# Feed-forward down product: one sum over the inner dimension in eight PSUM banks, in place of Strassen groups

## The chip, the cores and the metric

The kernel runs on one core of a Trainium2 chip. The core has five engines that run beside one another: TensorE (PE) multiplies matrices, VectorE (DVE) and ScalarE (ACT) do elementwise work, GpSimd (POOL) does so too, and SyncE (SP) issues transfers. A matmul's result goes to PSUM, which has eight banks of 128 x 512 floats; everything else lies in SBUF, in tiles of 128 partitions. The metric is the device time of one execution in microseconds.

## The reference

Two layers, each a token mixer and a feed-forward block with a normalised residual after both. Only the feed-forward block is touched:

```python
def layer_norm(x, g, b, eps=LN_EPS):
    mu = x.mean(-1, keepdims=True)
    var = jnp.square(x - mu).mean(-1, keepdims=True)
    return (x - mu) * lax.rsqrt(var + eps) * g + b

def conv_ffn(x, w_up, conv_w, conv_b, w_down):
    S = x.shape[1]
    u = x @ w_up
    up = jnp.pad(u, ((0, 0), (CONV_W - 1, 0), (0, 0)))
    u = sum(up[:, j:j + S] * conv_w[j] for j in range(CONV_W)) + conv_b
    gate, val = jnp.split(u, 2, axis=-1)
    return (jax.nn.silu(gate) * val) @ w_down

for i in range(2):
    x = layer_norm(ALPHA * x + mixer[i](x), ...)          # RWKV, then sparse attention
    x = layer_norm(ALPHA * x + conv_ffn(x, ...), ...)
```

There are 1024 tokens, the model dimension is 1024 and the inner dimension of the feed-forward block 2816, which is 22 blocks of 128 or 11 pairs of blocks. All values are float32. The product at issue is the last one, silu(gate) * val (1024 x 2816) times w_down (2816 x 1024).

## The kernel before

The program has four phases, one after the other: RWKV mixer, feed-forward block of layer 0, sparse attention, feed-forward block of layer 1 (L1948 to L1953). Each is a generator, and `drive` (L1956) lets the next phase begin its first steps between the last steps of the one before. The order of the instructions on each engine and the places of the tiles are set by a scheduler from the order in which the code names them, from the pools' buffer counts and from estimates of its own.

A product in float32 precision is made of three matmuls (`mm3`, L63 to L67): each operand is split into a high part, which ScalarE casts (`split`, L54), and a low part, the rest, which VectorE or GpSimd subtracts (L60). L65 multiplies high by high, L66 and L67 high by low and low by high. A matmul has a 128 x 128 stationary operand and a 128 x 512 moving one.

In the feed-forward block the up product comes first (`up`, L1019, itself in Strassen form), then per block the convolution and the gate on ScalarE and VectorE (`conv` L1041, `gated` L1055). The gated values go to a scratch in DRAM, `hd`, one 512 KB block of 128 x 1024 for each inner block.

Then comes the down phase. Before, it takes the pairs in groups: three, three, two and two pairs in layer 0, and three times three in layer 1. Inside a pair the two blocks, the two halves of the tokens and the two halves of the columns form the 2 x 2 scheme of Strassen's product: seven products in place of eight. `d_load` brings a pair into a `raw` tile (L1146, L1147). `d_op` (L1152) makes the operands of one of the seven products with VectorE sums and differences (L1158, L919) and splits them into `dh` and `dl`. `down` makes the product for four token tiles and all pairs of the group in a bank, and `add_to` (L1177) adds the bank to `acc` in SBUF on VectorE. The inner blocks that no group holds, two in layer 0 and four in layer 1, are multiplied directly at the end (bank `dt`, tiles `to`), tile by tile, and each tile's last addition (L1271) is followed by its norm (`norm_store` L146, `layer_norm_rows` L80 to L111) and its store. The norm's reciprocal root (`lnrs`, L103) and its last products (L110, L111) are GpSimd's, L107 is ScalarE's, the rest VectorE's.

Buffers by tag: `big` has three places in pool P and four in L in layer 0, two and five in layer 1; `t` (`t4`) has twelve in P and six or seven in N; `bank` gives four PSUM banks from PX and four from PY.

Layer 0's block yields after its last group, and the attention phase's first work lies between the last tiles: it multiplies two weight matrices into `wqk` (loads `uk` L1330, evacuation L1341, split, stores L1345) and splits its projection's weight `win`. Its real start are the loads `xr` (L1321) of the rows that the feed-forward block has stored, their transposes (`pt`) and the first `win` matmul.

Of the kernel before, what the change touches and what calls it, by code (L numbers as in the profile page):

```python
# [7 lines left out]
F32 = mybir.dt.float32  # L8
# [6 lines left out]
D = 1024  # L15
# [879 lines left out]
def ffn(k, layer, src, dst):  # L895
# [236 lines left out]
            gated(f)  # L1132


    NPAIR = NF // 2
    cuts = [0, 3, 6, 8, 10] if layer == 0 else [0, 3, 6, 9]
    groups = [range(a, b) for a, b in zip(cuts, cuts[1:])]
    in_P = (0, 3, 4, 8, 9) if layer == 0 else (0, 3, 6, 8)
    tail = range(2 * cuts[-1], NF)
    acc = []  # L1140
    R = {}

    def d_load(p):
# [8 lines left out]
    def d_op(p, n, pool, lo_eng):  # L1152

        r = R[p]
        raw = r["raw"]
        if n == "S1":
            q = r["q"] = sm("q")
            nc.vector.tensor_tensor(q[:, 0], raw[:, 1], raw[:, 3], ALU.add)  # L1158
            sub(q[:, 1], raw[:, 5], raw[:, 4])
        elif n == "S2":  # L1160
            q = r["q"]
            sub(q[:, 0], q[:, 0], raw[:, 0])
            sub(q[:, 1], raw[:, 7], q[:, 1])
        elif n == "S3":
            sub(raw[:, 1:6:4], raw[:, 0:8:7], raw[:, 1:6:4])
        elif n == "S4":
            sub(raw[:, 2], raw[:, 2], r["q"][:, 0])
        elif n == "22":
            sub(raw[:, 6], raw[:, 6], r["q"][:, 1])
        hi, lo = t4("dh", F32R, pool, (128, 2, 512)), t4("dl", F32R, pool, (128, 2, 512))  # L1170
        r[n] = hi, lo
        at = {"11": slice(0, 5, 4), "12": slice(2, 7, 4), "S3": slice(1, 6, 4), "S4": slice(2, 8, 5), "22": slice(3, 7, 3)}
        split(k, raw[:, at[n]] if n in at else r["q"], hi, lo, "a", lo_eng)
# [5 lines left out]
    B_ = {}  # L1179

    def down(gi, n, tt):
        new = n in ("11", "12", "S1")
        x = n in ("11", "S2", "S3", "22")
        if new:
            B_[x, tt] = bank("dn", PX if x else PY)
        ps = B_[x, tt]
        tsl = slice(128 * tt, 128 * tt + 128)
        for j, p in enumerate(groups[gi]):
            hi, lo = R[p][n]
            mm3(  # L1190
                k, ps, (hi[:, 0, tsl], lo[:, 0, tsl]), (hi[:, 1], lo[:, 1]), new and j == 0,
                n in ("12", "S4", "22") and j == len(groups[gi]) - 1, skip_group_check=True,
            )
# [3 lines left out]
    for p in groups[0]:
        d_load(p)
    for hf in range(2):
        a = big("acc", L_, (128, 4, 1024), F32)  # L1200
        acc.append(a)
        for tt in range(4):
            nc.sync.dma_start(a[:, tt], src[(4 * hf + tt) * 128 : (4 * hf + tt + 1) * 128, :])
    ng = len(groups)
    dsteps = [(gi, n) for gi in range(ng) for n in ("11", "12", "S1", "S2", "S3", "S4", "22")]
    done = set()

    def d_ops(j):
        if j < len(dsteps) and j not in done:
            done.add(j)  # L1210
            gi, n = dsteps[j]
            for i, p in enumerate(groups[gi]):
                d_op(p, n, N_ if i == 2 else P_, CFG["dl0"][3 * j + i] if j < 3 else "v" if i == 2 and n in ("11", "12", "S4") else "p")

    hs = []

    def tail_op(f):

        if layer == 1 and f == NF - 1:
            room = [t4("to", F32R, N_) for _ in range(4)]  # L1220
        else:
            room = big("to", L_, (128, 4, 1024))
            room = [room[:, i] for i in range(4)]
        for i, ap in enumerate((hd[f // 2][f % 2], k.w_down[layer, f * 128 : (f + 1) * 128, :])):
            raw = t4("tr")
            nc.sync.dma_start(raw, ap)
            split(k, raw, room[2 * i], room[2 * i + 1], "a", "p")
        hs.append(room)

    late = [NF - CFG["gl"] + i for i in range(CFG["gl"])]  # L1230
    for j, (gi, n) in enumerate(dsteps):
        for x in CFG["ga"] if j == 0 else "":
            if x == "g":
                gated(late.pop(0))
            else:
                d_ops(int(x))
        d_ops(j)
        if n == "11" and gi + 1 < ng:
            for p in groups[gi + 1]:
                d_load(p)  # L1240
        d_ops(j + 1)
        if j == 0:
            while late:
                gated(late.pop(0))
        if gi == ng - 1 and n in ("S2", "S3", "S4") and (i := ("S2", "S3", "S4").index(n)) < len(tail):
            tail_op(tail[i])
        for tt in range(4):
            down(gi, n, tt)
    if len(tail) > 3:
        tail_op(tail[3])  # L1250
    lnw = []
    for z in range(2):
        if layer == 0:
            lnw.append(L_.tile([128, D], F32, name=f"lnw{z}"))
        else:
            lnw.append(sm("lnw").rearrange("p a b -> p (a b)"))
        i = B_LN + 4 * layer + 2 + z
        nc.sync.dma_start(lnw[z], k.bvec[i : i + 1, :].to_broadcast([128, D]))
# [3 lines left out]
    for tt in range(8):
        tsl = slice(128 * tt, 128 * tt + 128)
        r = [acc[tt // 4][:, tt % 4, 512 * ch : 512 * ch + 512] for ch in range(2)]
        sums = L_.tile([128, 2], F32, name="lns", tag="lns", bufs=2)
        for ch in range(2):
            cs = slice(512 * ch, 512 * ch + 512)
            ps = bank("dt")
            for i, (a, b, c, d) in enumerate(hs):
                mm3(k, ps, (a[:, tsl], b[:, tsl]), (c[:, cs], d[:, cs]), i == 0, i == len(hs) - 1)  # L1270
            nc.vector.scalar_tensor_tensor(  # L1271
                r[ch], r[ch], 1.0, ps, ALU.mult, ALU.add, accum_out=sums[:, ch : ch + 1]
            )
        kw = {} if layer else dict(sums=sums, junk=L_.tile([128, 512], BF16, name="lnj", tag="lnj", bufs=1))
        norm_store(k, L_, r, lnw, dst, 128 * tt, CFG["ln4"][layer] if tt < 7 else "pv", **kw)
# [711 lines left out]
```

## Time and profile before

| | us |
|---|---|
| median of 3 runs | 3228.42 (3226.88 to 3240.63) |
| the profiled execution | 3233.26 |
| its span on the core | 3231.4 |
| PE busy (15032 matmuls) | 2864.5, 89% |
| DVE busy | 2455.2, 76% |
| POOL busy | 1518.1, 47% |
| ACT busy | 1377.4, 43% |
| layer 0's down phase | about 1504 to 1805 |
| layer 1's down phase | about 2956 to 3231 |

The span is the time in which the core works; the rest of the execution's time lies around it. Times in the rows below count from the start of the span. A matmul's row says 0.39 us, since matmuls overlap in the array; the distance between starts is what one costs. "Idle before" in brackets is how long an engine waited ahead of an instruction and what released it. The granted clock is TensorE's as a share of its full 2.4 GHz.

### The profile page before, as it was taken

How to read it: one execution, taken by the hardware profiler on the slowest of the kernel's cores; microseconds unless marked ns; L12 is line 12 of the kernel's file. 1: busy time of each engine (PE TensorE's matmuls, PEld its weight loads, DVE VectorE, ACT ScalarE, POOL GpSimd, SP SyncE). 2: the span in 40 equal slices, each digit the busy share in tenths (PEclk: the TensorE clock that was granted, in tenths of full speed). 3: DMA queues.
4: the chain of work that ended last, by engine and by line, in shares of the span. 5: the costliest groups of instructions: out<-in, count | busy, mean ns of one | idle time of the engine just before them, and what ended most of it. 6: DMA issues, size and time to landing. Idle time of an engine off the chain costs nothing. (4 is left out here: it accounts for less than half of the span.)

```text
span 3231.4 us, 41664 instructions
## 1 busy us (share of the span) xinstructions
PE 2864.5 (89%) x15032; PEld 2246.0 (70%) x15032; DVE 2455.2 (76%) x3925; ACT 1377.4 (43%) x2363; POOL 1518.1 (47%) x987
## 2 busy tenths in 40 slices
PE   7689889989897899999698888888998899999788
PEld 3468657777675677777576766566787677777577
DVE  5486767766756788888976689997475888888975
ACT  3433234322322544444223577775363544444331
POOL 2433215222144667766767522212313677766766
PEclk9788978879898999999889889999999999999899
DMA  5554533534325222235212521112214222235212
GB/s 178 198 199 141 189 108 113 181 135 161 121 86 179 82 79 79 78 92 207 78 66 73 182 69 54 45 33 101 80 43 163 61 78 79 79 98 202 78 52 91
DMA packets 236224, 356.44 MB, mean 110 GB/s; under 512 B 17290, under 2 KB 110858, under 8 KB 235634
## 3 DMA queue, kind: packets, MB, share of 16 engines
q1 hardware_dynamic: 208370, 303.44, 29.3%
q10 hardware_dynamic: 27648, 50.34, 4.1%
q8 instruction: 118, 1.93, 0.3%
q14 instruction: 88, 0.72, 0.1%
HBM read 250.57 MB, written 103.15 MB: 109 GB/s over the span
## 5 line engine op out<-in xcount | busy, mean ns | idle before, releaser
L60 POOL TENSOR_TENSOR wo<-wr,wo 128x512 fp32r<-128x512 f32 x220 | 410.8, 1891 | 288.8 <-ACT wo L54 288.8
L1050 DVE SCALAR_TENSOR_TENSOR cv<-u,vec,cv 128x1023 f32<-128x1023 f32 (+1 forms) x176 | 348.2, 1996 | 52.9 <-ACT cv L1045 51.1
L65 PE MATMUL dn<-dh 128*128 128x512 f32 x532 | 219.4, 412 | 68.5 <-DVE acc L1177 68.4
L60 POOL TENSOR_TENSOR dl<-raw,dh 128x1024 fp32r<-128x1024 f32 x82 | 221.1, 2719 | 101.4 <-ACT dh L54 101.1
L65 PE MATMUL p<-xT,wo 128*128 128x512 f32 x528 | 213.4, 404 | 25.3 <-ACT u L1034 19.0
L66 PE MATMUL dn<-dl,dh 128*128 128x512 f32 x532 | 218.1, 410 | 15.2 <-POOL dl L60 7.7
L67 PE MATMUL dn<-dh,dl 128*128 128x512 f32 x532 | 215.9, 406 | 0.0
L1045 ACT ACTIVATE cv<-u,vec 128x1024 f32<-128x1024 f32 x88 | 109.5, 1244 | 248.8 <-DVE u L1039 248.2
L1682 POOL TENSOR_TENSOR cm<-sc,toep 128x256 f32<-128x256 f32 x96 | 75.7, 794 | 297.1 <-DVE mn L1698 228.5
L67 PE MATMUL p<-xT,wo 128*128 128x512 f32 x528 | 208.7, 395 | 5.1 <-POOL wo L60 5.1
L66 PE MATMUL p<-xT,wo 128*128 128x512 f32 x528 | 208.6, 395 | 3.0 <-DVE xT L60 3.0
L1177 DVE SCALAR_TENSOR_TENSOR acc<-acc,dn 128x512 f32<-128x512 f32 x196 | 130.8, 679 | 86.7 <-PE dn L67 86.7
L60 POOL TENSOR_TENSOR wo<-S,wo 128x512 fp32r<-128x512 f32 x88 | 175.6, 2014 | 30.3 <-ACT wo L54 30.3
L54 ACT CAST dh<-raw 128x1024 fp32r<-128x1024 f32 x95 | 94.8, 1047 | 198.0 <-PE dn L67 80.7
L65 PEld LDWEIGHTS dn<-dh 128*128 128x128 f32 x532 | 105.7, 199 | 98.0 <-DVE acc L1177 42.5
L60 POOL TENSOR_TENSOR wl<-wr,wh 128x512 fp32r<-128x512 f32 x56 | 76.6, 1367 | 199.2 <-ACT wh L54 118.5
L65 PEld LDWEIGHTS p<-xT,wo 128*128 128x128 f32 x528 | 100.6, 190 | 63.6 <-ACT u L1034 34.2
L65 PE MATMUL p<-x,wo 128*128 128x512 f32 x352 | 138.8, 394 | 2.8 <-DVE x L60 2.3
L54 ACT CAST wo<-wr 128x512 fp32r<-128x512 f32 x220 | 127.0, 618 | 29.1 <-POOL wo L60 18.7
L54 ACT CAST wh<-wr 128x512 fp32r<-128x512 f32 x108 | 66.6, 621 | 169.8 <-DMA wr<-in_w_w_dram 51.6
L66 PE MATMUL p<-x,wo 128*128 128x512 f32 x352 | 138.4, 393 | 0.0
L65 PE MATMUL pa<-xmh,wh 128*128 128x512 f32 x256 | 106.1, 439 | 36.3 <-ACT xmh L54 32.2
(422 smaller groups left out, 8685.9 us busy)
## 6 DMA issues: line engine op xcount, KB each, us to landing
wr<-in_w_up_dram SPq DMA_DIRECT2D x88, 512.0 KB, 5.9
hd<-cv SPq DMA_DIRECT2D x44, 512.0 KB, 3.4
raw<-hd SPq DMA_DIRECT2D x19, 1024.0 KB, 5.0
raw<-in_w_down_dram SPq DMA_DIRECT2D x19, 1024.0 KB, 7.7
wr<-in_w_wo_dram SPq DMA_DIRECT2D x68, 256.0 KB, 2.9
wr<-in_w_rkv_dram SPq DMA_DIRECT2D x48, 256.0 KB, 3.4
kept_w<-wh ACTq DMA_DIRECT2D x48, 256.0 KB, 2.2
kept_w<-wl ACTq DMA_DIRECT2D x48, 256.0 KB, 3.7
```

The lines of the kernel that those rows point to most:

```text
L54: nc.scalar.copy(hi, raw)
L60: eng.tensor_tensor(lo, raw, f32(hi), ALU.subtract)
L65: mm(ps, lhs[0], rhs[0], start=start, stop=False, **kw)
L66: mm(ps, lhs[0], rhs[1], start=False, stop=False, **kw)
L67: mm(ps, lhs[1], rhs[0], start=False, stop=stop, **kw)
L1045: nc.scalar.activation(o, u, AF.Identity, bias=k.vec[:, cb : cb + 1], scale=k.vec[:, cw[2] : cw[2] + 1])
L1050: nc.vector.scalar_tensor_tensor(o[:, d:], u[:, : 1024 - d], k.vec[:, cw[j] : cw[j] + 1], o[:, d:], ALU.mult, ALU.add)
L1177: nc.vector.scalar_tensor_tensor(o, o, ALPHA if first else 1.0, ps, ALU.mult, ALU.add)
L1682: (nc.vector if CFG["cm"][h4] == "v" else nc.gpsimd).tensor_tensor(cm[:, :near], mk, toep[g][:, h % 8, 256 - near :], ALU.add)
```

## The change

The Strassen groups, their operand sums, the additions of each bank to `acc` and the `dt` remainder go. The down product is made for half of the tokens at a time, `hf` 0 and 1. Eight banks hold the half's whole result: four token tiles times two column halves. A step is one pair `p`: for each of the eight banks two inner blocks times three matmuls, 48 matmuls. All 11 pairs are summed in the banks. The last two pairs of a half (`LAST`) are done bank by bank in `d_end`, whose addition (L1178 of the new kernel) brings the bank into SBUF together with ALPHA times the residual row; the norm of a tile follows when both of its banks are done.

`d_prep` makes the operands of a step two steps ahead: the half of the pair's gated values (`hr`, 512 KB; high part `hh` on ScalarE, low part `hl` on VectorE) and two blocks of w_down (`dr`, 512 KB each; high and low parts in one `wd` tile of tag `big`, on ScalarE and GpSimd). The weights are loaded and split once for each half, so twice in all. The last two pairs of the second half have their operands in pool L, the others in P. The norms of the first half's tiles lie under the first steps of the second half. In layer 0 the block yields to the attention phase once after the first four banks of the last `d_end`, four times behind it, and after each of the last four tiles.

```diff
-    cuts = [0, 3, 6, 8, 10] if layer == 0 else [0, 3, 6, 9]
-    groups = [range(a, b) for a, b in zip(cuts, cuts[1:])]
...
-    def add_to(hf, tt, ch, ps, first):
-        o = acc[hf][:, tt, 512 * ch : 512 * ch + 512]
-        nc.vector.scalar_tensor_tensor(o, o, ALPHA if first else 1.0, ps, ALU.mult, ALU.add)
...
+    NPAIR, LAST = NF // 2, 2
+    ops, hold, lnw, sums, rows = {}, {}, [], {}, {}
+
+    def d_prep(hf, p):
+
+        late = hf == 1 and p >= NPAIR - LAST
+        hr = t4("hr")
         nc.sync.dma_start(
...
+            hr.rearrange("p (f c) -> p f c", f=2), hd[p][:, :, 512 * hf : 512 * hf + 512].rearrange("f p c -> p f c")
         )
...
+        else:
+            h = t4("hh", F32R), t4("hl", F32R)
+        w = big("wd", L_ if late else P_, (128, 4, 1024))
+        split(k, hr, *h, "a", "v")
+        for f in range(2):
+            wr = t4("dr", pool=N_)
+            nc.sync.dma_start(wr, k.w_down[layer, (2 * p + f) * 128 : (2 * p + f + 1) * 128, :])
+            split(k, wr, w[:, 2 * f], w[:, 2 * f + 1], "a", "p")
+        ops[hf, p] = *h, w
+
+    def d_mm(ps, hf, p, tt, ch):
+        hh, hl, w = ops[hf, p]
+        for f in range(2):
+            ts = slice(512 * f + 128 * tt, 512 * f + 128 * tt + 128)
+            cs = slice(512 * ch, 512 * ch + 512)
             mm3(
+                k, ps, (hh[:, ts], hl[:, ts]), (w[:, 2 * f, cs], w[:, 2 * f + 1, cs]), p == f == 0,
+                p == NPAIR - 1 and f == 1,
             )
...
+    def d_end(ps, hf, tt, ch):
+
+        for p in range(NPAIR - LAST, NPAIR):
+            d_mm(ps, hf, p, tt, ch)
...
+        nc.vector.scalar_tensor_tensor(
+            r, r, ALPHA, ps, ALU.mult, ALU.add, accum_out=sums[hf, tt][:, ch : ch + 1]
+        )
...
+    steps = [(hf, p) for hf in range(2) for p in range(NPAIR)]
+    for s in steps[:2]:
+        d_prep(*s)
+    for f in range(NF - CFG["gl"], NF):
+        gated(f)
+    order = [(ch, tt) for ch in (1, 0) for tt in range(4)]
+    for i, (hf, p) in enumerate(steps):
+        if i + 2 < len(steps):
+            d_prep(*steps[i + 2])
+        if p == 0:
+            bk = {x: bank("dn", PX if x[0] == 0 else PY) for x in order}
+        if p < NPAIR - LAST:
+            for ch, tt in order:
+                d_mm(bk[ch, tt], hf, p, tt, ch)
...
+        if (hf, p) == (0, NPAIR - 1):
+            for ch, tt in order:
+                d_end(bk[ch, tt], 0, tt, ch)
+                if ch == 0:
+                    d_norm(0, tt)
+    for tt in range(4):
+        d_end(bk[1, tt], 1, tt, 1)
     if layer == 0:
         pools.close(P_, N_, PY)
         yield
...
+        for tt in range(4):
+            yield
+    for tt in range(4):
+        d_end(bk[0, tt], 1, tt, 0)
+        d_norm(1, tt)
         if layer == 0:
             yield
```

Three places show what stands on the engines. First VectorE in layer 1's down phase. Before, inside the last Strassen group:

```order
L60 TENSOR_TENSOR dl<-raw,dh 128x1024
L1177 SCALAR_TENSOR_TENSOR acc<-acc,dn 128x512 x6
L1158 TENSOR_TENSOR q<-raw 128x512
L1177 SCALAR_TENSOR_TENSOR acc<-acc,dn 128x512 x2
L919 TENSOR_TENSOR q<-raw 128x512
L919 TENSOR_TENSOR raw<-raw 128x2x512
L1177 SCALAR_TENSOR_TENSOR acc<-acc,dn 128x512
L60 TENSOR_TENSOR dl<-raw,dh 128x1024
L1177 SCALAR_TENSOR_TENSOR acc<-acc,dn 128x512 x3
L60 TENSOR_TENSOR dl<-raw,dh 128x1024
L1177 SCALAR_TENSOR_TENSOR acc<-acc,dn 128x512 x4
```

After, from the last gated blocks to the end of the first half:

```order
L60 TENSOR_TENSOR hl<-hr,hh 128x1024
L1059 TENSOR_TENSOR cv<-cv 128x1024
L1050 SCALAR_TENSOR_TENSOR cv<-u_23625,vec,cv 128x1023
L1050 SCALAR_TENSOR_TENSOR cv<-u_23625,vec,cv 128x1022
L1059 TENSOR_TENSOR cv<-cv 128x1024
L60 TENSOR_TENSOR hl<-hr,hh 128x1024 x11
L1178 SCALAR_TENSOR_TENSOR acc,lns<-acc,dn 128x512
L92 BN_STATS lnst<-acc 128x6
L1178 SCALAR_TENSOR_TENSOR acc,lns<-acc,dn 128x512 x4
L92 BN_STATS lnst<-acc 128x6 x2
```

The bank additions and Strassen sums between the products are gone; the low parts `hl` of eleven steps stand in one row, and the next bank is read at the half's end.

Second, GpSimd in layer 1, with the tiles' numbers. Before, at the end of the last group:

```order
L60 TENSOR_TENSOR dl_25133<-raw_24411,dh_25132 128x1024
L60 TENSOR_TENSOR to_25082<-tr_25083,to_25082 128x1024
L60 TENSOR_TENSOR to_25082<-tr_25087,to_25082 128x1024
L60 TENSOR_TENSOR dl_25138<-raw_24414,dh_25137 128x1024
L60 TENSOR_TENSOR to_25146<-tr_25147,to_25146 128x1024
L60 TENSOR_TENSOR to_25146<-tr_25151,to_25146 128x1024
L60 TENSOR_TENSOR to_25236<-tr_25239,to_25235 128x1024
L60 TENSOR_TENSOR to_25238<-tr_25243,to_25237 128x1024
L103 TENSOR_TENSOR lnrs_25281<-lnve_25280,mhalf_64 128x1
L110 TENSOR_TENSOR acc_23958<-acc_23958,lnw_25247 128x512
L111 TENSOR_TENSOR acc_23958<-acc_23958,lnw_25249 128x512
L103 TENSOR_TENSOR lnrs_25328<-lnve_25327,mhalf_64 128x1
```

After, from the last pair of the first half (`wd_24405`) to the first pairs of the second (`wd_24468`, `wd_24483`):

```order
L60 TENSOR_TENSOR wd_24405<-dr_24408,wd_24405 128x1024
L60 TENSOR_TENSOR wd_24405<-dr_24412,wd_24405 128x1024
L103 TENSOR_TENSOR lnrs_24564<-lnve_24563,mhalf_64 128x1
L110 TENSOR_TENSOR acc_24203<-acc_24203,lnw_24208 128x512
L111 TENSOR_TENSOR acc_24203<-acc_24203,lnw_24210 128x512
L103 TENSOR_TENSOR lnrs_24595<-lnve_24594,mhalf_64 128x1
L60 TENSOR_TENSOR wd_24468<-dr_24471,wd_24468 128x1024
L60 TENSOR_TENSOR wd_24468<-dr_24475,wd_24468 128x1024
L103 TENSOR_TENSOR lnrs_24626<-lnve_24625,mhalf_64 128x1
L60 TENSOR_TENSOR wd_24483<-dr_24486,wd_24483 128x1024
L60 TENSOR_TENSOR wd_24483<-dr_24490,wd_24483 128x1024
L110 TENSOR_TENSOR acc_24203<-acc_24203,lnw_24208 128x512
```

Norm work of the first half's tiles now stands between the low parts of the weights, where before it followed all of them.

Third, TensorE at the end of layer 0. Before, at the first `wqk` products:

```order
L67 MATMUL dt_13235<-to_12889 128x512
L65 MATMUL dt_13235<-to_12936 128x512
L66 MATMUL dt_13235<-to_12936 128x512
L67 MATMUL dt_13235<-to_12936 128x512
L1337 MATMUL wqk_13076<-uk_13074,uq_13072 128x128 x4
L1337 MATMUL wqk_13089<-uk_13074,uq_13072 128x128 x4
L1337 MATMUL wqk_13102<-uk_13074,uq_13072 128x128 x4
L1337 MATMUL wqk_13115<-uk_13074,uq_13072 128x128 x4
L65 MATMUL dt_13269<-to_12889 128x512
L66 MATMUL dt_13269<-to_12889 128x512
L67 MATMUL dt_13269<-to_12889 128x512
```

After:

```order
L65 MATMUL dn_12476<-wd_12914,hl_12913 128x512
L1292 MATMUL wqk_13123<-uk_13121,uq_13119 128x128 x4
L1292 MATMUL wqk_13136<-uk_13121,uq_13119 128x128 x4
L1292 MATMUL wqk_13149<-uk_13121,uq_13119 128x128 x4
L1292 MATMUL wqk_13162<-uk_13121,uq_13119 128x128 x4
L66 MATMUL dn_12476<-wd_12914,hl_12913 128x512
L67 MATMUL dn_12476<-wd_12914,hl_12913 128x512
L65 MATMUL dn_12476<-wd_12975,hl_12913 128x512
L66 MATMUL dn_12476<-wd_12975,hl_12913 128x512
L67 MATMUL dn_12476<-wd_12975,hl_12913 128x512
```

The same first `wqk` products stand in the fifth bank of the last `d_end`, where before they stood between the first two tiles of the remainder.

## Rows read from the trace of the kernel before

**Rows 1.** The windows: us, then busy us of PE, PEld, DVE, ACT, POOL, clock, DMA, GB/s
```profile
1100.00:1200.00 100.00, 97.07 (x421) 78.22 (x420) 89.13 (x64) 51.05 (x76) 69.67 (x36) 1.00 0.28 81
...
1550.00:1600.00 50.00, 36.84 (x156) 30.05 (x155) 42.02 (x37) 12.19 (x13) 31.46 (x13) 0.86 0.33 126
3000.00:3050.00 50.00, 37.61 (x159) 30.36 (x158) 44.07 (x38) 12.28 (x13) 33.12 (x12) 0.90 0.34 126
3170.00:3220.00 50.00, 50.00 (x223) 41.40 (x222) 34.78 (x82) 7.97 (x11) 31.93 (x23) 1.00 0.17 64
```

**Rows 2.** The waits of layer 0's down phase: us in total, times, longest
```profile
DVE acc L1177 <- PE dn L67: 44.6, 49, 2.4
ACT dh L54 <- PE dn L67: 43.4, 7, 20.2
...
PE dn L65 <- DVE acc L1177: 38.6, 8, 13.2
```

**Rows 3.** The waits of layer 1's down phase
```profile
ACT dh L54 <- PE dn L67: 56.3, 7, 20.0
...
PE dn L65 <- DVE acc L1177: 29.8, 6, 12.2
```

**Rows 4.** TensorE's timeline: start, us, engine, line, operation, tiles, idle before
```profile
1503.79 0.39 PE L65 MATMUL dn<-dh 128*128 128x512 f32 x1
...
1504.47 0.39 PE L65 MATMUL dn<-dh 128*128 128x512 f32 x1
...
1518.27 0.79 PE L66 MATMUL dn<-dl,dh 128*128 128x512 f32 x1 [4.57 <-DVE dl L60]
1518.86 0.63 PE L67 MATMUL dn<-dh,dl 128*128 128x512 f32 x1
1519.29 0.63 PE L65 MATMUL dn<-dh 128*128 128x512 f32 x1
...
1796.11 0.39 PE L67 MATMUL dt<-to 128*128 128x512 f32 x1
...
1805.26 0.73 PE L65 MATMUL win<-win,X 128*128 128x456 f32 x1
...
2956.21 0.39 PE L65 MATMUL dn<-dh 128*128 128x512 f32 x1
...
3221.75 0.39 PE L67 MATMUL dt<-to 128*128 128x512 f32 x1
```

**Rows 5.** The tiles dn and dt: count, duration min/median/max in ns, first and last start
```profile
L65 PE MATMUL dn<-dh x532: 387/389/796, 1503.8 to 3177.8; 128*128 128x512 f32 x178
...
L65 PE MATMUL dt<-to x96: 389/389/793, 1758.5 to 3221.3; 128*128 128x512 f32 x96
```

**Rows 6.** Low parts and casts of 128x1024, by tile and line: count, min/median/max in ns
```profile
L60 POOL TENSOR_TENSOR dl<-raw,dh x82: 2344/2782/3403, 1484.9 to 3166.6; 128x1024 fp32r<-128x1024 f32 x82
...
L60 DVE TENSOR_TENSOR dl<-raw,dh x13: 1210/2506/3386, 1514.8 to 3146.6; 128x1024 fp32r<-128x1024 f32 x13
...
L54 ACT CAST dh<-raw x95: 1031/1047/1057, 1483.1 to 3164.2; 128x1024 fp32r<-128x1024 f32 x95
```

**Rows 7.** The windows, just before layer 0's down phase
```profile
1480.00:1500.00 20.00, 20.00 (x90) 16.57 (x89) 13.78 (x13) 8.48 (x12) 10.66 (x6) 1.00 0.99 372
```

**Rows 8.** The timeline of TensorE and SyncE at the end of layer 0
```profile
1761.28 3.50 PE L1337 MATMUL wqk<-uk,uq 64*128 64x128 f32 x32
...
1775.90 0.42 SPq L1330 DMA_DIRECT2D uk<-in_w_uk_dram  x1
...
1796.58 0.32 SPq L1345 DMA_DIRECT2D wqk<-wqkl  x1
```

**Rows 9.** The timeline of the last tile's norm
```profile
3222.18 0.69 DVE L1271 SCALAR_TENSOR_TENSOR acc<-acc,dt 128x512 f32<-128x512 f32 x1 [0.32 <-PE dt L67]
...
3225.21 0.75 DVE L108 SCALAR_TENSOR_TENSOR acc<-acc,lnrs,lnw 128x512 f32<-128x512 f32 x1
...
3226.22 1.26 POOL L110 TENSOR_TENSOR acc<-acc,lnw 128x512 f32<-128x512 f32 x1 [1.12 <-ACT acc L107]
```

More of the change, by code (lines that the diff above doesn't have):

```diff
@@ L1147, in d_load @@
+    ops, hold, lnw, sums, rows = {}, {}, [], {}, {}
+    def d_prep(hf, p):
+        late = hf == 1 and p >= NPAIR - LAST
+        hr = t4("hr")
         nc.sync.dma_start(
-            raw[:, 4:8].rearrange("p (f a) c -> p f (a c)", f=2),
-            k.w_down[layer, p * 256 : (p + 1) * 256, :].rearrange("(f p) c -> p f c", p=128),
-        )
[L1152 to L1173, printed above, removed]
@@ L1197, in ffn @@
[L1197 to L1213, printed above, removed]
@@ L1215, in ffn @@
[L1215 to L1258, printed above, removed]
+            hr.rearrange("p (f c) -> p f c", f=2), hd[p][:, :, 512 * hf : 512 * hf + 512].rearrange("f p c -> p f c")
+        )
@@ new lines, in d_prep @@
+        if late:
+            if not hold:
+                hold["h"] = big("hl", L_, (128, 4, 1024))
+            i = 2 * (p - NPAIR + LAST)
+            h = hold["h"][:, i], hold["h"][:, i + 1]
+        else:
[6 more added lines that the diff above has]
+            split(k, wr, w[:, 2 * f], w[:, 2 * f + 1], "a", "p")
@@ new lines, in d_norm @@
+    def d_norm(hf, tt):
+        r = [rows[hf][:, tt, 512 * ch : 512 * ch + 512] for ch in range(2)]
+        kw = {} if layer else dict(
+            sums=sums[hf, tt], junk=L_.tile([128, 512], BF16, name="lnj", tag="lnj", bufs=1)
+        )
+        norm_store(
+            k, L_, r, lnw, dst, 128 * (4 * hf + tt), CFG["ln4"][layer] if (hf, tt) != (1, 3) else "pv", **kw
+        )
+    steps = [(hf, p) for hf in range(2) for p in range(NPAIR)]
[3 more added lines that the diff above has]
+        gated(f)
@@ new lines, in ffn @@
+    order = [(ch, tt) for ch in (1, 0) for tt in range(4)]
[7 more added lines that the diff above has]
+                d_mm(bk[ch, tt], hf, p, tt, ch)
+        if p == 4:
+            rows[hf] = big("acc", L_, (128, 4, 1024), F32)
+            for tt in range(4):
+                nc.sync.dma_start(rows[hf][:, tt], src[(4 * hf + tt) * 128 : (4 * hf + tt + 1) * 128, :])
+            for z in range(0 if lnw else 2):
+                if layer == 0:
+                    lnw.append(L_.tile([128, D], F32, name=f"lnw{z}"))
+                else:
+                    lnw.append(sm("lnw").rearrange("p a b -> p (a b)"))
+                i_ = B_LN + 4 * layer + 2 + z
+                nc.sync.dma_start(lnw[z], k.bvec[i_ : i_ + 1, :].to_broadcast([128, D]))
+        if (hf, p) == (0, NPAIR - 1):
[3 more added lines that the diff above has]
+                    d_norm(0, tt)
@@ L1261, in ffn @@
         yield
[L1262 to L1275, printed above, removed]
+        for tt in range(4):
+            yield
+    for tt in range(4):
+        d_end(bk[0, tt], 1, tt, 0)
+        d_norm(1, tt)
         if layer == 0:
```

26 lines of the change are left out of this document (3 added, 23 removed).

## The prediction

> **What bounds the kernel now.** I read the table of windows first, then the waits of the two feed-forward down phases, then single TensorE rows. In the up phase (the stage before each down phase) TensorE is busy 97.07 of 100 us at a granted clock of 1.00. In the down phases it drops to 36.84 of 50 us at 0.86 in layer 0 and 37.61 of 50 at 0.90 in layer 1, and no other engine is full there in both (VectorE 42.02 and 44.07, GpSimd 31.46 and 33.12) [rows 1]. So a chain and not an engine sets the pace. The waits name it: TensorE waits for the VectorE add that brings a bank into SBUF (L1177: 38.6 us in layer 0, 29.8 in layer 1); VectorE waits at that add for the last matmul (44.6 us); ScalarE waits before the next operand cast for the matmuls that still read the buffer (43.4 and 56.3) [rows 2, 3]. It is a circle: matmul, add, Strassen sum, cast, low part, matmul.
>
> How much it loses: three matmuls start 0.68 us after three (1503.79 to 1504.47), so 0.2267 each when nothing is missing; after an idle 4.57 us they start 0.43 apart instead (1518.86 to 1519.29), TensorE's lower level (1.2 in place of 2.4 GHz) [rows 4]. The down phases hold 3 x 532 "dn" and 3 x 96 "dt" matmuls [rows 5]; by the code's groups 840 + 96 = 936 in layer 0 and 756 + 192 = 948 in layer 1. Dense they would take 212.2 and 214.9 us. Layer 0 takes 301.5 from its first (1503.79) to the first matmul of the attention projection that follows (1805.26); layer 1 takes 265.5 from 2956.21 to its last start at 3221.75 [rows 4]. Lost: 89 us (7 of them two batches of the attention phase's own "wqk" matmuls, 3.50 each [rows 8]) and 51 us.
>
> **The change part by part.** *More matmuls.* 11 steps of 48 for each half is 1056 per layer: 120 and 108 more than now. At 0.2267 that is 239.4 us per layer, +27.2 and +24.5, all on the path.
>
> *The circle goes.* A step is 48 matmuls, 10.88 us, into eight banks that nobody reads before the half's end, so no add and no bank stands between steps; the 196 adds of L1177 become 16 per layer. What remains is operand preparation, which must stay under 10.88 us a step. ScalarE: three casts of 1.05 = 3.1. VectorE: one low part, 1.2 to 3.4. GpSimd: two low parts of 2.78, 5.6, and 6.8 if both are the longest [rows 6]. All fit. Layer 0 has three weight slots, so preparation runs a whole step ahead. Layer 1 has two: the weights of step i+2 may be cast only when step i's last matmul is done and must be ready 10.88 us later; the chain is 1.05 + 2 x (2.34 to 3.40) = 5.7 to 7.9, which leaves 3 to 5 us. I cost it at nothing; if that cover fails, rival A has the price. Each step loads 1.57 MB in 10.88 us, 145 GB/s; the queue moved 372 GB/s in a stretch just before layer 0's down phase [rows 7]. The doubled weight loads therefore cost nothing on the path.
>
> A sentence apart, on a rule against this: the Trainium skill, "TensorE: Matmul & The Clock Gate", section "A second HAM failure mode: psum-queue depth-cycling", tells of a kernel that cycled through PSUM banks and in which TensorE paused so often between groups that its clock oscillated. By that rule the eight-bank cycle would keep today's clock, which is rival B. This trace speaks against it for dense matmuls: the "dt" matmuls of 3170 to 3220 change bank every 12 and ran 50.00 of 50 us at 1.00 [rows 1].
>
> *Start of each phase.* In layer 0 the operands of steps 0 and 1 are made under the last up products and step 2's has a free slot; the idle 4.57 us goes, and I take no stall. In layer 1 step 2's weights need step 0's slot: free at 2956.2 + 10.9 = 2967.1, ready 5.7 to 7.9 later, wanted at 2978.0. No stall; up to 3.5 if convolution work ahead on VectorE and ScalarE delays the load.
>
> *Middle, between the halves.* In layer 1 both slots belong to the last two pairs, whose 96 matmuls run bank by bank for 21.8 us, so the first is free only 1.4 us before the end. One cast and two low parts (1.05 + 4.7 to 5.6) end 4.4 to 5.3 us behind the last matmul; the products that need only high parts come first and cover a part. That is about 4.5 us idle, and then ten matmuls 0.2 us longer each at the lower level [rows 4], 2. Behind it GpSimd has six additions of the norm at 1.26 [rows 9] and one root between the second and the third weight block, which eats nearly all of that block's slack: 0 to 5, I take 0.5. Sum 7, bounds 0 and 12. Layer 0 has the third slot, and the next weights are ready before the half ends: 0.
>
> *End of layer 1.* Now the last tile's chain starts with its add at 3222.18, has VectorE to 3225.96, GpSimd's addition at 3226.22 [rows 9] and ends with the span at 3231.4: 9.3 behind the last matmul. After, TensorE needs 12 x 0.2267 = 2.72 us per tile, VectorE about the 3.78 of that chain and up to 4.1 with the other column half. Four tiles start 8.2 us before the last matmul ends, the last add starts 3.2 to 4.1 behind it, and the end comes 12.4 to 14.8 behind (the long end if tiles wait for one another on GpSimd). I take 13.5.
>
> Layer 1: 2956.2 + 239.4 + 7 + 13.5 = 3216.1 against 3231.4: a gain of 15.
>
> *End of layer 0.* The last 96 matmuls start at 1503.8 + 960 x 0.2267 = 1721.4. The attention phase starts behind a chain: first "wqk" products, four evacuations with split and store, the load of the second "uk" on SyncE behind those stores (1775.90), four more products, stores up to 1796.58, and only behind them on SyncE the loads of the rows. From first "wqk" (1761.28) to the first projection matmul (1805.26) it took 44.0 us [rows 4, 8], interleaved with the norms of eight tiles. After, the order puts the first "wqk" 52 matmuls into the last 96: 1721.4 + 11.8 = 1733.2, with the norms of four tiles in the chain. If it keeps its 44.0, the projection starts at 1777 (gain 28). If the chain hid wholly, TensorE's own work ends at 1721.4 + 21.8 + 2 x 3.5 = 1750 and the loads and transposes add the 8.8 that lie between 1796.5 and 1805.26: 1759 (gain 46). Half of the norm work leaves the chain, so I take the middle of what stays, 33 us: 1766, a gain of 39. Everything behind it moves up by that.
>
> **Sum.** 39 + 15 = 54 us. Against the profiled execution (3233.3) that is 3179; this run lies 4.8 above the median shown, 3228.4, and I carry the difference: **3174**. With the bounds of the costs (28 to 46, and 9 to 23) the forecast's own range is 3160 to 3192.
>
> **The rivals.** *A: preparation in layer 1's two slots is late each step.* For: the slot makes cast and low parts serial behind the last matmul, and the low part has a longest of 3.40 on GpSimd [rows 6]. Against: that still fits. If load landings and queues make each of 18 steps 1.5 us late: 27 us, 3201. With the worse end of layer 0's chain (28 in place of 39) as well: 3212, no change that a measurement could tell.
> *B, slower: the clock stays where it is.* Mechanism: at each step's first matmuls TensorE waits shortly for low parts, and its granted clock stays at the 0.86 now seen in layer 0 [rows 1]. The 2 x 239.4 = 478.8 us would take 478.8 / 0.86 = 556.7, +78: 3252. It decides from a mean clock of 0.90 (478.8 / 0.90 is +53, the whole gain), which is layer 1's present value. Against: the pauses would have to recur in steps whose preparation has 3 us and more to spare.
> *C: the end of layer 0 keeps its 44 us chain*, because stores and loads on SyncE pace it and not the norms: gain 28 + 15 = 43, 3185, in the forecast's range.
> *That the change doesn't do what it says* can be left out: the order shows the steps without an add between them.
>
> **How the numbers follow.** 0.5% (16 us) is about what a measurement of this kernel can tell from no change. Forecast 0.62 and C 0.14 (together 3160 to 3192), A alone 0.12 (3201), A with C 0.05 (3212), B 0.07 (3252). Faster 0.62 + 0.14 + 0.12 = 0.88, but at the edges of A a part falls within 0.5%: 0.86; same 0.07; slower 0.07. To hold 8 in 10 the range runs from 3158 to 3204: A with C, B and a little of A lie above.
>
> **What would show it.** Right: in the windows of both down phases TensorE busy 49 of 50 at clock 0.98 or more; no wait for L1177's successor inside a half; one gap of some 4 us on TensorE in the middle of layer 1's phase, with GpSimd as releaser, and none in layer 0's; first "win" matmul near 1766; some 13 us from last matmul to end. Wrong: gaps every 10.88 us with the weights' low part as releaser (A), a clock below 0.95 in the windows (B), the first "win" at 1777 (C).

## The result and the profile after

The changed kernel takes 3192.28 us (median of 4 runs, 3187.91 to 3196.08), the kernel before 3227.65 (median of 4, 3223.84 to 3240.63): a ratio of 0.9883, with a 95% interval of 0.9852 to 0.9914. Faster by 1.2%, some 35 us (median against median), where 54 were forecast. The profiled execution took 3196.08, with a span of 3194.3 against 3231.4.

The two traces are best compared by stretches between four marks: the first down matmul of layer 0, the first projection matmul of the attention phase, the first down matmul of layer 1, and the end of the span. In the table "ahead" is what lies ahead of the first mark.

| us | before | after | forecast |
|---|---|---|---|
| ahead | 1503.8 | 1503.2 | 1503.8 |
| layer 0's down phase, to the first projection matmul | 301.5 | 268.8 | 262.5 |
| attention phase and layer 1's up phase | 1150.9 | 1151.7 | 1150.9 |
| layer 1's down phase, to the end | 275.2 | 270.6 | 259.9 |

The gain is layer 0's: 32.7 of the 37 us by which the spans differ. Layer 1 gives 4.6 where 15 were expected. The same view of windows as [rows 1], of the changed kernel:

```profile
1550.00:1600.00 50.00, 50.00 (x223) 41.40 (x222) 6.15 (x5) 14.90 (x15) 24.36 (x11) 1.00 0.51 172
1743.00:1770.00 27.00, 8.37 (x54) 7.04 (x53) 11.21 (x29) 11.98 (x25) 17.38 (x16) 0.74 0.59 209
...
3035.00:3085.00 50.00, 42.28 (x170) 32.91 (x169) 28.62 (x40) 11.86 (x13) 29.76 (x18) 0.93 0.43 147
3085.00:3135.00 50.00, 50.00 (x223) 41.38 (x222) 6.14 (x5) 18.36 (x20) 33.25 (x14) 1.00 0.37 127
```

While a half runs, TensorE is busy 50.00 of 50 us at a granted clock of 1.00; what was 0.86 in [rows 1] is gone. Two stretches stand out: the end of layer 0 (1743 to 1770), where it is busy 8.37 of 27 us, and the middle of layer 1 (3035 to 3085), where it is busy 42.28 of 50 at a clock of 0.93. TensorE's waits in layer 0's down phase (engine, line, releaser; total, times, longest):

```profile
PE pt L1323 <- DMA xr<-x: 16.7, 1, 16.7
```

Neither the bank additions nor low parts of operands appear any more. The 38.6 us of [rows 2] are gone; what is left is one wait of 16.7 for the attention phase's row loads, where the kernel before waited 5.0 for them, and one of 1.9 for the second `uk` load. In layer 1:

```profile
PE dn L66 <- POOL wd L60: 8.2, 6, 2.0
PE dn L65 <- ACT wd L54: 1.9, 1, 1.9
```

The 29.8 us of [rows 3] are gone too; 10.1 came in their place. Where they lie, by TensorE's timeline (start, us, operation; in brackets the idle time before it and its releaser):

```profile
3025.64 0.50 PE L66 MATMUL dn<-wd,hh 128*128 128x512 f32 x1 [1.25 <-POOL wd L60]
...
3027.96 0.50 PE L66 MATMUL dn<-wd,hh 128*128 128x512 f32 x1 [1.13 <-POOL wd L60]
...
3049.48 0.50 PE L66 MATMUL dn<-wd,hh 128*128 128x512 f32 x1 [1.61 <-POOL wd L60]
...
3051.81 0.50 PE L66 MATMUL dn<-wd,hh 128*128 128x512 f32 x1 [1.14 <-POOL wd L60]
...
3073.95 0.50 PE L65 MATMUL dn<-wd,hh 128*128 128x512 f32 x1 [1.90 <-ACT wd L54]
3076.47 0.50 PE L66 MATMUL dn<-wd,hh 128*128 128x512 f32 x1 [2.02 <-POOL wd L60]
...
3078.78 0.79 PE L66 MATMUL dn<-wd,hh 128*128 128x512 f32 x1 [1.05 <-POOL wd L60]
...
3083.22 0.63 PE L67 MATMUL dn<-wd,hl 128*128 128x512 f32 x1
```

There are three places. What a place costs is the time from a matmul ahead of it to one behind it, less 0.2267 us for each matmul between. At 3025.64 and 3027.96, in the first banks of the first half's bank-by-bank end, it is 3.1. At 3049.48 and 3051.81, at the start of the second half, it is 3.4. At 3073.95, 3076.47 and 3078.78, two steps later, it is 6.0 (5.8 at the three waits), and 2.5 more for the matmuls behind, which start 0.43 us apart in place of 0.2267 (rows of 0.63 us, the last at 3083.22). Sum 15.0; the view of waits counts only the idle time in it. The expectations below put the three at 2.9, 3.8 and 7.8: those figures take a row that stands for two or four matmuls (x2, x4) as one.

### The profile page after: what moved, and what is told of

The parts are those of the page before. It is cut to its first block, busy times and chain, and to the rows that moved or that the text cites. A ratio compares the mean times of both kernels' runs of the same rounds, so it can differ in the third digit from the quotient of the medians.

```text
span 3194.3 us, 41814 instructions
## 1 busy us (share of the span) xinstructions
PE 2881.4 (90%) x15260; PEld 2266.8 (71%) x15260; DVE 2160.8 (68%) x3627; ACT 1367.9 (43%) x2350; POOL 1384.5 (43%) x943
## 5 line engine op out<-in xcount | busy, mean ns | idle before, releaser
L60 POOL TENSOR_TENSOR wd<-dr,wd 128x1024 fp32r<-128x1024 f32 x88 | 218.2, 2505 | 170.1 <-ACT wd L54 170.1
L67 PE MATMUL dn<-wd,hl 128*128 128x512 f32 x704 | 275.1, 391 | 0.0
L66 PE MATMUL dn<-wd,hh 128*128 128x512 f32 x640 | 250.9, 392 | 8.2 <-POOL wd L60 8.2
L65 PE MATMUL dn<-wd,hh 128*128 128x512 f32 x640 | 249.6, 391 | 1.9 <-ACT wd L54 1.9
L1045 ACT ACTIVATE cv<-u,vec 128x1024 f32<-128x1024 f32 x88 | 109.5, 1245 | 239.1 <-DVE u L1039 238.9
L60 DVE TENSOR_TENSOR hl<-hr,hh 128x1024 fp32r<-128x1024 f32 x40 | 58.6, 1464 | 207.0 <-ACT hh L54 93.9
L67 PEld LDWEIGHTS dn<-wd,hl 128*128 128x128 f32 x704 | 132.7, 189 | 27.5
L66 PEld LDWEIGHTS dn<-wd,hh 128*128 128x128 f32 x640 | 120.7, 189 | 36.2 <-POOL wd L60 11.3
L65 PEld LDWEIGHTS dn<-wd,hh 128*128 128x128 f32 x640 | 120.6, 189 | 27.9 <-ACT wd L54 2.8
L65 PE MATMUL p<-x,wo 128*128 128x512 f32 x352 | 139.1, 395 | 1.2 <-DVE x L60 0.7
L54 ACT CAST wd<-dr 128x1024 fp32r<-128x1024 f32 x88 | 88.7, 1049 | 117.0 <-PE dn L67 63.9
```

The source lines that it names most:

```text
L54: nc.scalar.copy(hi, raw)
L60: eng.tensor_tensor(lo, raw, f32(hi), ALU.subtract)
L65: mm(ps, lhs[0], rhs[0], start=start, stop=False, **kw)
L66: mm(ps, lhs[0], rhs[1], start=False, stop=False, **kw)
L67: mm(ps, lhs[1], rhs[0], start=False, stop=stop, **kw)
L1045: nc.scalar.activation(o, u, AF.Identity, bias=k.vec[:, cb : cb + 1], scale=k.vec[:, cw[2] : cw[2] + 1])
```

## Experiments

The start of the first down matmul differs between the profiles by up to 18 us (1497.97 in one, 1516.46 in another), though the kernels share the phase ahead of it, and the total time differs with it. So the experiments are read by the stretches above, which repeat within 2 us or so where a kernel leaves them alone: layer 0's down phase was 268.5 to 268.8 us in all six profiles that have it as in the changed kernel, and 301.5 and 299.8 in the two that have it as before. Three kernels ran only once (the cast moved 3199.08 us, one pair 3196.22, twice the transfers 3193.32); they are read by their stretches alone. The theory after the result: layer 0 pays nearly all; its rest is a chain of stores and loads on SyncE; in layer 1 two weight slots and the order on ScalarE and SyncE make the three gaps. The rivals: both layers gain alike; GpSimd's norm additions or the doubled transfers make the gaps.

**One layer at a time.** The Strassen code is kept for one of the two layers:

```diff
+    if layer == 1:            # in the other kernel: layer == 0
+        ... the Strassen down phase of the kernel before ...
+        return
     NPAIR, LAST = NF // 2, 2
```

> The new down phase in layer 0 alone, Strassen groups kept in layer 1. Theory (nearly all of the 35 us comes from layer 0, where the first projection matmul moved from 1805.26 to 1771.96, 33.3 us): about 3195 us. Rival (both layers gain alike, and what layer 0 shows is partly given back later): about 3210 us.

> The new down phase in layer 1 alone, Strassen groups kept in layer 0. Theory (layer 1's phase from its first matmul to the end shrank only from 275 to 270.6 us): about 3223 us, a difference that a measurement can hardly tell from none. Rival (both layers gain alike): about 3210 us.

Measured: layer 0 alone 3195.47 us, 0.990 (0.987 to 0.993) of the kernel before; layer 1 alone 3226.16, 0.999 (0.997 to 1.001). Layer 0's phase is 268.7 in the first; layer 1's phase is 271.6 in the second, and 274.6 with Strassen groups in the first. So layer 0 pays alone, and in layer 1 the change as made is worth 3 to 5 us, which the times can't tell from nothing.

**The load of the third step.** In layer 1 that step's three loads (`hr` and both `dr` of step (1, 2), the second half's third) are issued before the first half's norms, and `d_prep` takes them from there:

```diff
+        if layer == 1 and (hf, p) == (0, NPAIR - 1):
+            raws_[1, 2] = d_load(1, 2)
         if (hf, p) == (0, NPAIR - 1):
             for ch, tt in order:
                 d_end(bk[ch, tt], 0, tt, ch)
```

> As the changed kernel, but in layer 1 the loads of the second half's third step are issued before the norms and stores of the first half. Theory (the gap of 7.8 us at that step comes from the activation load that stands behind seven output stores on SyncE, and with it the weights' cast behind the activation's cast on ScalarE): TensorE's gap there falls to 1 to 1.5 us, the gaps at the half's end (2.9) and behind it (3.8) stay, and the time falls by about 6.5 us to 3186. Rival (GpSimd's norm additions hold the low parts up): the gap stays above 4 us.

A miss: 3196.85 us, layer 1's phase 274.0, and the gap is still 5.4 us (2.05, 2.30 and 1.06). That is what the rival expected too, so the gap's size does not tell the two apart; the rows do. I had moved the wrong load. SyncE and ScalarE of this run:

```profile
3070.39 7.86 SPq L149 DMA_DIRECT2D out_dram<-acc  x4
3078.34 0.41 SPq L1145 DMA_DIRECT2D hr<-hd  x1
...
3082.88 1.04 ACT L54 CAST hh<-hr 128x1024 fp32r<-128x1024 f32 x1 [4.81 <-DMA hr<-hd]
```

The load at 3078.34 behind four output stores is that of the step two later, (1, 4), and ScalarE's cast at 3082.88 has waited for it. The third step's own activations had long been loaded and cast. But ScalarE's order puts the cast of step (1, 4)'s activations ahead of the third step's weight casts, and these wait for nothing else. The changed kernel reads the same way (SyncE, ScalarE and GpSimd):

```profile
3059.41 7.85 SPq L149 DMA_DIRECT2D out_dram<-acc  x4
3067.35 0.40 SPq L1143 DMA_DIRECT2D hr<-hd  x1
...
3071.90 1.04 ACT L54 CAST hh<-hr 128x1024 fp32r<-128x1024 f32 x1 [4.81 <-DMA hr<-hd]
3072.86 1.99 ACT L54 CAST wd<-dr 128x1024 fp32r<-128x1024 f32 x2
...
3068.53 1.29 POOL L111 TENSOR_TENSOR acc<-acc,lnw 128x512 f32<-128x512 f32 x1
3073.97 4.76 POOL L60 TENSOR_TENSOR wd<-dr,wd 128x1024 fp32r<-128x1024 f32 x2 [4.15 <-ACT wd L54]
```

The stores hold SyncE until 3067.26, the load follows at 3067.35 and lands for the cast at 3071.90; the weight casts come behind it at 3072.86, and GpSimd, which had finished its norm additions at 3069.8, starts the low parts at 3073.97. What the stores waited for stands in SyncE's waits from 3059 to 3068:

```profile
SPq L149 <- POOL acc L111: 6.0, 2, 3.0
SPq L149 <- DVE acc L108: 5.7, 2, 5.4
```

So the norm of the first half, on GpSimd and VectorE, also stands at the head of the late load.

**That cast on another engine.** The next experiment takes only this cast out of ScalarE's row:

```diff
-        split(k, hr, *h, "a", "v")
+        split(k, hr, *h, "v" if layer == 1 and (hf, p) == (1, 4) else "a", "v")
```

> As the changed kernel, but in layer 1 the high part of the activations of one step, the second half's fifth, is cast on VectorE in place of ScalarE. Theory (the weights' casts of the third step stand behind this cast on ScalarE, which waits for a load behind the output stores): TensorE's gap of 5.8 us at the third step, with the lower clock behind it, falls to about 2, which GpSimd's norm additions leave; the gaps at the half's end and behind it stay. Rival (GpSimd's additions alone make the gap): it stays above 4 us.

```profile
3077.48 0.50 PE L66 MATMUL dn<-wd,hh 128*128 128x512 f32 x1 [1.80 <-POOL wd L60]
...
3089.87 0.50 PE L66 MATMUL dn<-wd,hh 128*128 128x512 f32 x1 [1.89 <-POOL wd L60]
...
3093.15 0.80 PE L66 MATMUL dn<-wd,hh 128*128 128x512 f32 x1 [2.01 <-POOL wd L60]
...
3069.45 1.98 ACT L54 CAST wd<-dr 128x1024 fp32r<-128x1024 f32 x2
3081.33 1.05 ACT L54 CAST hh<-hr 128x1024 fp32r<-128x1024 f32 x1 [9.89 <-DMA hr<-hd]
...
3086.24 1.99 ACT L54 CAST wd<-dr 128x1024 fp32r<-128x1024 f32 x2
```

As the theory said, the weight casts now run at 3069.45, the gap at the third step is 1.96 us (start 3077.48) where it was 5.8, and what is left is GpSimd behind its norm additions. But the next step shows the same thing again: ScalarE's cast at 3081.33 has waited 9.89 us for another activation load, the weight casts of step (1, 3) stand behind it at 3086.24, and TensorE waits at 3089.87 and 3093.15. The phase is 273.0 us, no shorter; some 1.6 us of that are a lower clock behind the two waits at the half's end, which this edit does not touch (last section). So the order on ScalarE behind late loads is shown to be the larger cause of the third gap; taking one cast out moves the wait to the next step.

**One pair at the half's end.** In layer 1's first half only the last pair is done bank by bank:

```diff
+    def last(hf):
+        return 1 if layer == 1 and hf == 0 else LAST
...
-        for p in range(NPAIR - LAST, NPAIR):
+        for p in range(NPAIR - last(hf), NPAIR):
...
-        if p < NPAIR - LAST:
+        if p < NPAIR - last(hf):
```

> As the changed kernel, but in layer 1's first half only the last pair is done bank by bank, in place of the last two. Theory (bank by bank, the last pair's weights are wanted 1.4 us behind the release of their slot, in place of 10.9): the gaps at the half's end (2.9 us) go, and those right behind it (3.8) shrink or go, since the slot of the second half's first weights comes free 10.9 us earlier; the gap at the third step stays. Rival (it is not the slot but GpSimd's pace): the gaps at the half's end stay.

```profile
3061.38 0.50 PE L65 MATMUL dn<-wd,hh 128*128 128x512 f32 x1 [1.75 <-DVE acc L1181]
...
3076.77 0.69 PE L66 MATMUL dn<-wd,hh 128*128 128x512 f32 x1 [2.62 <-POOL wd L60]
...
3079.09 0.79 PE L66 MATMUL dn<-wd,hh 128*128 128x512 f32 x1 [0.77 <-POOL wd L60]
```

Both gaps at the half's end and both behind it are gone. A new one of 1.9 us stands at 3061.38: with half as many matmuls to a bank the next half reaches a bank before VectorE has read it. At the third step 4.0 are left (2.78 and 1.18), or 6.7 with the matmuls at the lower clock around them, where it was 8.5. The phase is 264.1 us against 270.6. The gaps that went are those that the theory named; the third, which it left as it was, shrank a little.

**A third slot.** In layer 1 every third weight tile goes to pool L, whose places are free by then:

```diff
-        w = big("wd", L_ if late else P_, (128, 4, 1024))
+        w = big("wd", L_ if late or layer == 1 and (NPAIR * hf + p) % 3 == 2 else P_, (128, 4, 1024))
```

> As the changed kernel, but in layer 1 every third step has its weights in a slot of pool L, three slots in turn as in layer 0. Theory (with two slots the last pair's weights and the second half's first weights come too late): the gaps at the half's end (2.9 us) and behind it (3.8 us) go, the gap of 7.8 us two steps later stays, since the load behind the output stores stays; time about 6.5 us lower, 3186. Rival (transfers or GpSimd set these gaps): they stay, and so does the time, 3192.

3177.78 us, 0.984 (0.981 to 0.987) of the kernel before. That interval still touches the changed kernel's (0.985 to 0.991); the stretch decides. The window of layer 1's down phase over the half's boundary:

```profile
3020.00:3070.00 50.00, 50.00 (x223) 41.39 (x222) 29.47 (x47) 11.86 (x13) 30.01 (x18) 1.00 0.42 144
```

TensorE is dense from the first down matmul (2918.99) to the last (start 3158.12): 239.1 us, what 1056 matmuls were said to cost. All three gaps are gone, the third too, where I had expected it to stay: with a slot free earlier the third step's weight casts (3042.17) are put ahead of the activation cast of step (1, 4) that waits for its load (3062.93). ScalarE:

```profile
3042.17 1.98 ACT L54 CAST wd<-dr 128x1024 fp32r<-128x1024 f32 x2
...
3062.93 1.05 ACT L54 CAST hh<-hr 128x1024 fp32r<-128x1024 f32 x1 [3.67 <-DMA hr<-hd]
```

So the late load only hurts where the missing slot has pushed the weight casts behind it. The phase is 255.4 us, 15.2 less than in the changed kernel, which is what the three gaps cost (15.0).

**The row loads at layer 0's end.** The attention phase loads the rows of the first half's four tiles before its weight products, into one of its large buffers:

```diff
+            if tt == 0:
+                held.append(f32(big("xr", (128, 2, 8, 256)).rearrange("p a b c -> p (a b c)")))
-            xr = u("xr")
+            xr = held[0][:, 1024 * tt + 512 * g : 1024 * tt + 512 * g + 512] if tt < 4 else u("xr")
...
+    for tt in range(4):
+        x_load(tt)
     wqk = k.dram.tile([8, 2, 128, 512], F32, name="wqk")
```

> As the changed kernel, but the attention phase loads the first four row tiles, which the first half has stored long before, ahead of its weight products and into a buffer of its own. Theory (at layer 0's end TensorE waits 16.7 us for row loads that stand on SyncE behind the stores of the weight products): the first projection matmul comes about 253 us behind the first down matmul in place of 268.8, and the time falls by about 15 us to 3177. Rival (the wait only moves, to the fifth row tile or to the weight products' consumers): the first projection matmul comes earlier, but the time stays within 4 us of 3192.

```profile
1761.46 5.66 PE L1298 MATMUL wqk<-uk,uq 64*128 64x128 f32 x32 [3.17 <-DMA uk<-in_w_uk_dram]
1767.05 1.97 PE L1329 MATMUL pt<-ident,xr 128*128 128x128 f32 x8
...
1772.03 0.44 PE L65 MATMUL win<-win,X 128*128 128x456 f32 x1 [0.61 <-DVE X L1335]
```

The first projection matmul comes at 1772.03, 255.6 us behind the first down matmul (1516.46) in place of 268.8, right behind the transposes and with no wait for the rows. Of the wait of 16.7 us 13.2 are won; the second "wqk" products now wait 3.17 for their load and run slowly (5.66 us in place of 3.47, the granted clock 0.61 from 1761 to 1767). The stretch behind stays at 1151.5, so the 13 us are kept. The times do not show it: the median is 3183.91, 8 us below the changed kernel's, but the kernel before, measured beside it, came out lower too (3223.54), and the ratio is the same 0.988 (0.985 to 0.991). This profile had the longest stretch ahead of all, 1516.5.

**Twice the transfers.** On the kernel with three slots each block of w_down is loaded a second time into a buffer that nobody reads:

```diff
+            again = t4("dr2", pool=N_)
+            nc.sync.dma_start(again, k.w_down[layer, (2 * p + f) * 128 : (2 * p + f + 1) * 128, :])
```

> As the kernel with three weight slots in layer 1, but every block of w_down is loaded a second time into a buffer that nobody reads, 1 MB more per step. Theory (transfers have room: the weights' second load costs nothing on the path): no gap of TensorE in layer 1's down phase, from its first matmul to the last some 239 us, to the end some 255 us as before. Rival (the doubled weight loads were at the edge of the transfers): gaps at each step, and the phase some 10 us longer or more.

```profile
1520.00:1700.00 180.00, 176.42 (x770) 145.08 (x769) 58.12 (x63) 59.94 (x70) 96.26 (x45) 0.99 0.77 283
2960.00:3160.00 200.00, 198.65 (x876) 163.89 (x875) 58.47 (x67) 59.31 (x59) 111.34 (x50) 1.00 0.71 267
```

Layer 1's phase is 257.3 us (255.4 without) with one gap of 1.5 us; layer 0's is 274.2 (268.7), where the theory named layer 1 alone. With the DMA engines' share at 0.71 to 0.77 and 267 to 283 GB/s the cover begins to give (this run does not separate the engines' rate from the longer queue on SyncE), but the load that the change itself adds is hidden: in the kernel with three slots TensorE has no wait at all among the down matmuls of either layer.

**All together.** The third slot, the early row loads, and in layer 1's second half the last four pairs bank by bank in place of two:

```diff
+    def last(hf):
+        return 4 if layer == 1 and hf == 1 else LAST
...
+        third = layer == 1 and (i % 3 == 2 or i == 21)
...
-        w = big("wd", L_ if late else P_, (128, 4, 1024))
+        w = big("wd", L_ if late or third else P_, (128, 4, 1024))
```

> Three changes together: every third weight block of layer 1 in pool L, the attention phase's first row loads early, and in layer 1's second half the last four pairs done bank by bank in place of two, so that each of the last tiles has 5.4 us of matmuls over its norm in place of 2.7. Theory: the first saves 15 us, the second 15, the third about 6 of the 15.9 us behind the last matmul; about 3156 us. Rival (what one saves the next phase loses): 3170 or more.

3152.99 us (median of 5, 3148.19 to 3157.15), 0.978 (0.975 to 0.981) of the kernel before, below both kernels. Layer 0's phase is 256.3 us and layer 1's 248.6. The rival, 3170 or more, did not come about. The last matmul:

```profile
3144.74 0.39 PE L67 MATMUL dn<-wd,hl 128*128 128x512 f32 x1
```

The span ends at 3154.2, 9.1 us behind the last matmul's end (3145.13), where the changed kernel needs 15.9.

## Why the prediction was right and where not

**What held.** The circle went, and the clock with it: 50.00 of 50 us at 1.00 in the middle of a half. Rival B, today's clock kept, did not come about. The Trainium skill's section "A second HAM failure mode: psum-queue depth-cycling" ("TensorE: Matmul & The Clock Gate") tells of a kernel that cycles through PSUM banks and pauses between its groups of matmuls often enough for the clock to oscillate. Here, with eight banks in turn every 10.88 us, the trace shows no pause between banks (50.00 of 50 us busy), and the clock stays: cycling alone does not bring it about. The matmul term was right to the microsecond: 239.1 us where a phase runs dense. Preparation inside a half is hidden in this run, also with two slots. ScalarE and GpSimd in a steady step of layer 1, and at the half's end:

```profile
3000.33 2.00 ACT L54 CAST wd<-dr 128x1024 fp32r<-128x1024 f32 x2 [6.15 <-PE dn L67]
...
3022.09 2.00 ACT L54 CAST wd<-dr 128x1024 fp32r<-128x1024 f32 x2 [6.18 <-PE dn L67]
...
3001.46 4.75 POOL L60 TENSOR_TENSOR wd<-dr,wd 128x1024 fp32r<-128x1024 f32 x2 [6.12 <-ACT wd L54]
...
3023.22 4.69 POOL L60 TENSOR_TENSOR wd<-dr,wd 128x1024 fp32r<-128x1024 f32 x2 [6.04 <-ACT wd L54]
```

From the slot's release (3000.33) to the end of both low parts (3006.21) it is 5.9 us of the 10.88, at the short end of the 5.7 to 7.9 taken from [rows 6]: with VectorE nearly idle a low part on GpSimd took 2.38 us. Rival A, a late step each time, did not come about. Layer 0, with its third slot, has no gap, as predicted.

**The term that failed most: the middle of layer 1.** It was put at 7 us, bounds 0 and 12, and measured 15.0, outside them.
- One part was left out: the half's own end. "Ready 10.88 us later" holds for steps, but in the bank-by-bank end the last pair is wanted six matmuls after the pair before it. Its slot is freed at 3022.09 (last rows above), its low parts run from 3023.22 to 3027.91, and TensorE loses 3.1 us. The experiment with one pair took this away.
- The start of the second half was put at 4.5 and 2 for the clock; it took 3.4, and the clock stayed (1.00 from 3049 to 3058).
- The third step was put at 0.5, bounds 0 and 5, with GpSimd's norm additions as the cause. It took 6.0 and 2.5 for the clock. The additions in GpSimd's own row are only the smaller cause (about 2, by the experiment with the cast moved); the larger is the order on ScalarE, a weight cast behind an activation cast whose load stands behind output stores on SyncE, which in turn wait for the norm. The prediction looked at the wait that the change adds on GpSimd and not at what is queued on the two engines ahead of it.

**The end of layer 1** was put at 13.5 us, bounds 12.4 and 14.8, and took 15.9 (last matmul, VectorE's last addition, and VectorE's two waits behind it):

```profile
3178.04 0.39 PE L67 MATMUL dn<-wd,hl 128*128 128x512 f32 x1
...
3180.12 0.63 DVE L1178 SCALAR_TENSOR_TENSOR acc<-acc,dn 128x512 f32<-128x512 f32 x1
...
3183.41 0.16 DVE L104 SCALAR_TENSOR_TENSOR lnnm<-lnmv,lnrs 128x1 f32<-128x1 f32 x1 [1.66 <-POOL lnrs L103]
...
3188.18 0.16 DVE L104 SCALAR_TENSOR_TENSOR lnnm<-lnmv,lnrs 128x1 f32<-128x1 f32 x1 [1.66 <-POOL lnrs L103]
```

The tiles wait for one another, as the long end of the range supposed, but longer: two reciprocal roots on GpSimd stand behind the additions of the tile before, and VectorE waited 1.66 us for each. The last addition itself was early, 1.7 us behind the last matmul where 3.2 to 4.1 were supposed; the way from it to the end took 14.2 us, where in the kernel before it took 9.2. With four pairs in the end there was time enough: 9.1 us.

**The end of layer 0** was put at a chain of 33 us from the first "wqk" products to the projection, gain 39; it took 39.3, gain 32.7, between forecast and rival C. TensorE and SyncE:

```profile
1732.63 3.50 PE L1292 MATMUL wqk<-uk,uq 64*128 64x128 f32 x32
...
1745.96 3.47 PE L1292 MATMUL wqk<-uk,uq 64*128 64x128 f32 x32 [1.89 <-DMA uk<-in_w_uk_dram]
...
1768.66 3.65 PE L1323 MATMUL pt<-ident,xr 128*128 128x128 f32 x16 [16.74 <-DMA xr<-x]
1771.96 0.73 PE L65 MATMUL win<-win,X 128*128 128x456 f32 x1
...
1743.05 0.41 SPq L1285 DMA_DIRECT2D uk<-in_w_uk_dram  x1
...
1762.87 0.32 SPq L1300 DMA_DIRECT2D wqk<-wqkl  x1
...
1763.74 1.41 SPq L1276 DMA_DIRECT2D xr<-x  x3
```

The first products came where the order put them (1732.63, predicted 1733.2), the second load at 1743.05. The step that failed is "half of the norm work leaves the chain": the first four products and their stores took 10.0 us (to 1742.64) without norms between, but the norms of the last four tiles all fell on the second four, and from 1745.96 to the last store it took 16.9. On GpSimd six additions of the norm (1745.70 to 1758.69) stand ahead of and between the low parts of these products (1751.59 to 1759.92), for which SyncE's stores wait, and on SyncE five stores of rows stand among them. TensorE itself was done with its matmuls at 1751.92 and waited 16.7. The early row loads show that it was this queue and not the rows: they are stored long before. Rival C named the right place, the stores and loads on SyncE; but by these rows the norms do delay those stores. No run took the norms away, so how much of the 16.9 is theirs stays open.

**The sum.** 39 and 15 became 32.7 and 4.6; the median 3192 lies inside the range of 3158 to 3204 and at the very edge of the forecast's own, 3160 to 3192. That it lies there is in part luck: layer 1's gain of 4.6 is below its own bounds of 9 to 23, and only because layer 0 did better than its worst does the sum still come near. Both errors go the same way and are much alike: stretches behind a boundary were costed by one engine's work, and most of what they lost was set by queues that hold several things in order.

## What to carry to other kernels

Accumulating in PSUM over the whole inner dimension can beat a scheme with an eighth fewer products when that scheme's operand sums and evacuations keep TensorE waiting; what it costs in matmuls was known here to the microsecond beforehand, what it saves depends on buffers at the boundaries. Count the buffers for the step with the shortest notice (the half's end, 1.4 us) and not for the steady step. And ask of each queue which instruction with a late input stands ahead of one whose input is there: here an activation cast ahead of a weight cast, and weight stores ahead of row loads, cost some 4 and 13 us.

## What was not expected of the hardware

The phase ahead of the first down matmul varies by 18 us between the profiles (1497.97 to 1516.46), much more than the stretches behind it, which repeat within about 2 us; why, no run here shows.

Pauses alike in all that the rows show did not always have the same sequel. In the changed kernel the two waits at the half's end (1.25 and 1.13 us idle) and the two at the second half's start (1.61 and 1.14) left TensorE's granted clock at 1.00; the three at the third step (1.90, 2.02 and 1.05) were followed by matmuls 0.43 us apart, at a granted clock of 0.50 from 3079 to 3083. But in the kernel with the cast moved the same two waits at the half's end (1.25 and 1.12) were followed by a clock of 0.50 from 3029 to 3032, and so it was with the loads issued early. The second wait in the kernel with the cast moved:

```profile
3028.88 0.79 PE L66 MATMUL dn<-wd,hh 128*128 128x512 f32 x1 [1.12 <-POOL wd L60]
```

So the number of pauses does not decide it, and such a gap cost some 1.5 us more in one run than in another.
